# A recurrent decoder step on one core: the samples' own tokens in one product for four heads, the normalizers of four heads together, the sums of squares one step later, and another order inside the residual

## The chip, the core and the metric

The kernel runs on one core of one Trainium2 chip. The metric is the device time of one execution in microseconds; here it is the median of several executions. TensorE (PE) multiplies matrices, VectorE (DVE), ScalarE (ACT) and GpSimd (POOL) work element by element, and SyncE (SP) and POOL issue most of the DMA transfers. Matmuls accumulate in PSUM; all other tiles lie in SBUF. PE has two rows in a profile: PE for matmuls and PEld for loading the stationary operand, which overlaps with them.

## The reference, cut to what matters

One layer of a decoder runs for a prompt of 256 tokens and for 8 sample sequences of 4 tokens each, with shared weights. Three branches run side by side: a linear recurrence (RG-LRU), gated linear attention (GLA, 4 heads) and mLSTM (4 heads); then comes an MLP. Everything is fp32.

```python
xn = rmsnorm(x, g_norm1) * (1.0 + sc1) + sh1
proj = xn @ w_in                       # 2048 -> all branches and the three merge gates
# GLA, per chunk (a sample sequence is one chunk of 4 tokens):
o = einsum(qe, S) + einsum(where(mask, qe @ ke^T, 0), v)
# mLSTM, per chunk:
num = ci * einsum(q, C) + einsum(S, v)
den = ci * einsum(q, n) + sum(S)
h = num / maximum(abs(den), exp(-mt))
merged = gate0 * (y_lru @ w_br_lru) + gate1 * (y_gla @ w_br_gla) + gate2 * (y_ml @ w_br_ml)
x = x + gt1 * (merged @ w_out)
x = x + gt2 * (square(relu(norm2(x) @ w_ff1)) @ w_ff2)
y = rmsnorm(x, g_final)
```

For a sample, the first term of `o` and of `num` (and `den`) reads the sequence's stored state, another one for each of the 8 sequences and 4 heads; the second term is the attention of the 4 new tokens to themselves, called *own tokens* below. `gt1` and `gt2` come, with four more factors, from a product of the conditioning vectors with `w_ada`.

## The kernel before, in words

Activations lie with features on the 128 partitions and tokens along the free axis: 256 prompt tokens and 32 sample tokens, 288 columns in all. Each large product streams its weights from HBM in tiles of 128 x 1024 elements (512 KB). ACT rounds a tile to its high half `hi` (L178), DVE subtracts to get the low half `lo` (L185), and PE runs three single-pass matmuls of 288 columns for each 128x128 block: hi by high activations (L211), hi by low activations (L212), lo by high activations (L213). `stream_` does this; it yields after each weight tile, which is one *group* of 24 such matmuls.

`run` drives such a stream. After each group it does one letter of a pattern set by `every` (its `skip` leaves out so many groups first; the pattern then repeats) and then one step of each generator in the list `side`. `L` loads one *unit*, a slice of `w_ada`, into one of the places named in `slots`; `V` visits: PE multiplies all loaded units (L366, with 32 output partitions for each of four quarters). Both the visit and the side steps are issued on PE behind the group's last matmul. Within these constraints a planner of the compiler sets the order of instructions on each engine; only SP's order is as written. POOL issues the DMAs of the sample states.

Two generators matter here. `gla` runs beside the first gate and merge, `mlstm` beside the second merge (`merge(1)`, 48 groups) and the two streams that make `mo` (16 groups); what is left of `mlstm` runs beside the first gate stream of `merge(2)` (8 groups), whose first branch product needs its result `yml`. Both end in a table `at` of steps, filled by `do(step, function)`.

In both, `pair` handles two loaded tiles of sample states. It makes one product with the states, sixteen PE instructions with each sequence's output on its own quarter of the partitions (L1114, L1517), accumulating in a tile from `longp` (pool `pi`, one buffer). It also adds the own tokens of that head: one matmul on partitions 0 to 31 (L1115 with `asb` in GLA for each head, L1520 with `psb` in mLSTM for each head's first pair). Then `update` forms the new states (L1126 and L1130; L1533 and L1536) in tiles from `misc` (pool `px`, two buffers), and ACT copies the finished output out of PSUM (L1119, L1525) into the tile `os`. A later step, `gather_tokens` (L939, L940), brings it back to features on partitions. In mLSTM, `gather` also spreads each head's normalizer, column 256, over the partitions: DVE multiplies it into an identity (L1544), PE multiplies that by ones (L1546, 32 columns), and DVE copies 32x32 of it into `den` (L1548). `squares` (L1554, L1557) squares the result, `last` prepares `den`, `head_sums` (L924) sums the squares over a head on PE, and DVE and ACT make scaling rows of it (`inv_sqrt`, `head_rows`); `scaled_rows` applies them (L142 on PE, L932 on DVE) and splits y into its halves (L556, L557).

`resid` adds a gated product to the residual: a long DVE instruction for the 256 prompt columns (L1643), a product of 32 sample columns into a small tile (L1646) and its addition (L1648). It is called 16 times behind `w_out` and 32 times in the MLP. In the last block of the MLP its result is squared (L495) and summed by PE (L499, L504), then scaled and written out (L1752, L1756).

Of the kernel before, what the change touches and what calls it, by code (L numbers as in the profile page):

```python
# [11 lines left out]
ALU = mybir.AluOpType  # L12
AX = mybir.AxisListType

P = 128
D = 2048
KT = D // P
NP = 256
NB = 8
TS = 4  # L20
NS = NB * TS
N = NP + NS
# [31 lines left out]
def trunk(ctx, tc, io):  # L54
# [28 lines left out]
    def misc():  # L83
        return px.tile([P, 512], F32, tag="px", name=nm("px"))

    def longp():
        return pi.tile([P, 512], F32, tag="pi", name=nm("pi"))

    def sc(shape, tag, bufs=2):
        return sp.tile(shape, F32, tag=tag, name=nm(tag), bufs=bufs)  # L90
# [14 lines left out]
    ident, eye = C("ident"), C("eye")  # L105
# [156 lines left out]
    def every(p, skip=0):  # L262

        pace.update(every=p.split(), n=-skip)
# [662 lines left out]
    def scaled_rows(y, z, r, h):  # L927
# [4 lines left out]
        V.tensor_tensor(out=z[:, a], in0=z[:, a], in1=p[:, :N].unsqueeze(1).to_broadcast([P, 2, N]), op=ALU.mult)  # L932
        split(y[0][:, a], y[1][:, a], z[:, a])

    def gather_tokens(dst, h, o):

        p = misc()
        for e in range(2):
            T.matmul(p[:, NS * e:NS * e + NS], o[:, e * P:(e + 1) * P], eye, start=True, stop=True)  # L939
        V.tensor_copy(dst[:, 2 * h:2 * h + 2, NP:N], p[:, 0:2 * NS].rearrange("p (e t) -> p e t", e=2))  # L940

    def gla():
# [142 lines left out]
        gn = sc([P, 2], "gn5", 1)  # L1085
        V.tensor_scalar(gn, Pm("gn"), 0.5, None, ALU.mult)
        y = []
        tiles, vxs, pos = {}, {}, {}

        def first():  # L1090
            parts(kp, ks, kr)
# [13 lines left out]
            spread(vxs[h], vp[:, h], half)  # L1105

        def pair(h):
            pos[h] = po = longp()
            ns = (2 * h, 2 * h + 1)
            s4s = [tiles[n][:, 0:1024].rearrange("p (b e) -> p b e", b=4) for n in ns]  # L1110
            for q in (1, 0):
                for j in range(4):
                    b = 4 * q + j
                    T.matmul(po[32 * j:32 * j + 32, 0:256], qm[:, h, NS * b:NS * b + NS], s4s[q][:, j, :], start=q == 1, stop=q == 0, skip_group_check=True)  # L1114
            T.matmul(po[0:32, 0:256], asb[:, h], vs[:, 0:256], start=False, stop=True, skip_group_check=True)  # L1115
            for q, s4 in enumerate(s4s):
                update(h, q, s4)
            pos[h] = sc([P, 257], "os", 1)
            S.copy(pos[h][:, 0:256], po[:, 0:256])  # L1119

        def update(h, q, s4):
            n = 2 * h + q
# [191 lines left out]
    def mlstm():  # L1314
# [161 lines left out]
        mn = sc([P, 2], "gn5", 1)  # L1476
        V.tensor_scalar(mn, Pm("mn"), 0.5, None, ALU.mult)
        sums = row("rr")
        tiles, vxs, pos, sqs, stores = {}, {}, {}, [], []
        v2 = flat(slot(2, F32R))  # L1480
        vx = v2[:, 0:1024].rearrange("p (b e) -> p b e", b=4)
        kps = kp, v2[:, 1024:2048].rearrange("p (h d) -> p h d", h=4)
# [22 lines left out]

        def pair(n):
            h = n // 4
            if n % 4 == 0:
                pos[h] = longp()
            po = pos[h]  # L1510
            s4s = [tiles[n + a].rearrange("p (b d e) -> p b d e", b=2, d=2) for a in range(2)]
            for a in (1, 0):
                q = n % 4 + a
                for i in range(2):
                    for d in range(2):
                        b, j = 2 * q + i, 2 * i + d
                        T.matmul(po[32 * j:32 * j + 32, 0:257], qm[:, 2 * h + d, NS * b:NS * b + NS], s4s[a][:, i, d, :],  # L1517
                                 start=q == 1, stop=q == 2, skip_group_check=True)
            if n % 4 == 0:
                T.matmul(po[0:32, 0:257], psb[:, h], vs, start=False, stop=False, skip_group_check=True)  # L1520
            for a, s4 in enumerate(s4s):
                update(n + a, s4)
            if n % 4:
                pos[h] = sc([P, 257], "os", 1)
                S.copy(pos[h], po[:, 0:257])  # L1525

        def update(n, s4):
            h, q = n // 4, n % 4
# [11 lines left out]

        def gather(h):
            gather_tokens(nT, h, pos[h])
            rd = sc([P, NS], "rd", 1)
            V.tensor_scalar(rd, eye, pos[h][:, 256:257], None, ALU.mult)  # L1544
            p = misc()
            T.matmul(p[:, 0:NS], ones, rd, start=True, stop=True)  # L1546
            r = slice(32 * h, 32 * h + 32)
            V.tensor_copy(den[r, NP:N], p[r, 0:NS])  # L1548

        def squares(h):  # L1550
            if not sqs:
# [9 lines left out]
        def do(s, f, *a):  # L1561
            at.setdefault(s, []).append(lambda: f(*a))
# [28 lines left out]
            V.scalar_tensor_tensor(den, den, EPS, den, ALU.mult, ALU.mult)  # L1591

        do(e + 2, last)
        do(e + 3, lambda: head_sums(sums, sqs[0]))
        do(e + 4, lambda: V.scalar_tensor_tensor(sums, sums, 1.0 / 256, den, ALU.mult, ALU.add))
        rows = []
        do(e + 4, lambda: rows.append(head_rows(inv_sqrt(sums, sums), v2)))
        yield from steps(at)
        while not mos:
            yield  # L1600
# [11 lines left out]

    merge(1, ygla, io["wbg"])
    slots.update(ids=(None, 8), n=0)
    every("L L . V . . .", skip=5)

    mo = slot(3)
    for b in range(2):
# [2 lines left out]
        run(stream(win, B_MO + b, act1, KT, ev_mo))  # L1621
    mos.append(mo)

    visit()
    slots.update(ids=(None, "st", 5), n=0)
    every(". L L L V . .", skip=6)
    merge(2, yml, io["wbm"])


# [10 lines left out]
        return mrg[k // 8][:, k % 8, :], mrg[2 + k // 8][:, k % 8, :]  # L1640

    def resid(x, z, kind, k):
        V.scalar_tensor_tensor(x[:, 0:NP], z[:, 0:NP], mod[:, kind, k, 0:1], x[:, 0:NP], ALU.mult, ALU.add)  # L1643
        t = sc([P, NS], "rs_t", 2)
        bc = [P, NB, TS]
        V.tensor_tensor(out=t.rearrange("p (b t) -> p b t", b=NB), in0=z[:, NP:N].rearrange("p (b t) -> p b t", b=NB),  # L1646
                        in1=mod[:, kind, k, 1:9].unsqueeze(2).to_broadcast(bc), op=ALU.mult)
        V.tensor_tensor(out=x[:, NP:N], in0=x[:, NP:N], in1=t, op=ALU.add)  # L1648

    xf = (slot(6), slot(7))  # L1650
# [227 lines left out]
```

## Time and profile before

| | us |
|---|---|
| median of 3 executions | 1930.77 (1930.58 to 1931.68) |
| the profiled execution | 1930.15 |
| its span, first to last instruction | 1928.0 |
| PE busy | 1907.8 |
| PEld busy | 1823.2 |
| DVE busy | 1035.3 |
| ACT busy | 806.2 |
| POOL busy | 250.4 |

The profiled execution's own time has some 2 us around the span. Busy times of an engine are added over its instructions. Bars of PE overlap, since the ends of matmuls are modelled. The three streaming lines L211 to L213 make up most of PE's time; the units' line L366 and the lines of the three branches are the rest. The groups that the change touches, with their number of instructions, busy us and mean ns:

| line | what | instructions | busy us | mean ns |
|---|---|---|---|---|
| L1115 | GLA's own tokens | 8 | 2.4 | 379 |
| L1520 | mLSTM's own tokens | 8 | 2.4 | 380 |
| L1546 | normalizers | 8 | 1.2 | 232 |
| L924 | sums of squares, both layers | 32 | 2.4 | 412 |

An fp32 matmul appears as two instructions, so four matmuls are eight.

### The profile page before, as it was taken

Reading aid. Unit: us, or ns where it says so; the run is one execution under the profiler, and the core shown is the slowest. Engines: PE = TensorE matmul, PEld = TensorE weight load, DVE = VectorE, ACT = ScalarE, POOL = GpSimd, SP = SyncE. Lnnn points to the kernel's source line nnn. Section 1 sums busy time; section 2 is a strip of 40 time slices with the busy share of each in tenths; the row PEclk is TensorE's granted clock in tenths of the full one; section 3 lists DMA queues with packets and bytes.
Section 4 is the critical chain, followed back from the end, with each engine's and each line's share of the span. In section 5 each row is a group of like instructions: output and inputs, shape, how many; then the busy total and the mean of one; then the engine's idle time right before and its main releaser. Section 6 shows DMA issues by size and latency. Waiting matters only on the chain.

```text
span 1928.0 us, 35983 instructions
## 1 busy us (share of the span) xinstructions
PE 1907.8 (99%) x15092; PEld 1823.2 (95%) x15092; DVE 1035.3 (54%) x1595; ACT 806.2 (42%) x1125; POOL 250.4 (13%) x350
## 2 busy tenths in 40 slices
PE   8999999999999999999999999999999999999997
PEld 6898999999999999899999899999999999999997
DVE  6666647546673456644454654345454544444565
ACT  4333465343554343343333444443333333343433
POOL 0000101021051222001122421010000000000101
PEclk9999999999999999999999999999999999999999
DMA  9997847558443569767788364544444445444452
GB/s 386 389 349 274 313 160 262 202 198 292 163 156 112 174 224 322 270 247 283 277 328 328 132 215 146 172 168 165 169 163 170 165 152 178 166 164 171 156 175 105
DMA packets 110402, 416.42 MB, mean 216 GB/s; under 512 B 11713, under 2 KB 12273, under 8 KB 106529
## 3 DMA queue, kind: packets, MB, share of 16 engines
q1 hardware_dynamic: 100992, 381.40, 55.4%
q0 software_dynamic: 8096, 29.19, 4.2%
q10 hardware_dynamic: 1152, 3.54, 0.5%
q8 instruction: 118, 1.93, 0.4%
q14 instruction: 44, 0.35, 0.1%
HBM read 397.27 MB, written 16.81 MB: 215 GB/s over the span
## 4 chain that ended last, share of the span: by engine, by line
PE 98%; DVE 1%; DMA 1%; ACT 0%; SPq 0%; issue 0%; DVEq 0%; ACTq 0%
PE mm L211 29%; PE mm L213 29%; PE mm L212 29%; PE pa L366 5%; DMA s<-wad 1%; PE px L1533 0%; PE px L769 0%; PE pi L1517 0%; PE px L1052 0%; PE px L1446 0%; PE px L1456 0%; PE mm L248 0%; PE pi L1070 0%; PE px L1126 0%; PE pi L504 0%; PE mm L249 0%
## 5 line engine op out<-in xcount | busy, mean ns | idle before, releaser
L185 DVE TENSOR_TENSOR lo<-raw,hi 128x1024 fp32r<-128x1024 f32 x448 | 548.4, 1226 | 536.5 <-ACT hi L178 514.0
L178 ACT ACTIVATE hi<-raw 128x1024 fp32r<-128x1024 f32 x444 | 470.2, 1060 | 779.6 <-PE mm L212 646.4
L211 PE MATMUL mm<-xh,hi 128*128 128x288 f32 x2528 | 743.9, 298 | 0.1
L212 PE MATMUL mm<-xl,hi 128*128 128x288 f32 x2528 | 741.9, 296 | 0.0
L213 PE MATMUL mm<-xh,lo 128*128 128x288 f32 x2528 | 731.9, 295 | 0.7 <-DVE lo L185 0.6
L211 PE MATMUL mm<-s,hi 128*128 128x288 f32 x1664 | 490.1, 297 | 0.0
L212 PE MATMUL mm<-s,hi 128*128 128x288 f32 x1664 | 488.6, 295 | 0.0
L211 PEld LDWEIGHTS mm<-xh,hi 128*128 128x128 f32 x2528 | 471.6, 188 | 16.2 <-issue 10.5
L213 PE MATMUL mm<-s,lo 128*128 128x288 f32 x1664 | 477.3, 295 | 0.0
L212 PEld LDWEIGHTS mm<-xl,hi 128*128 128x128 f32 x2528 | 474.1, 188 | 1.0
L213 PEld LDWEIGHTS mm<-xh,lo 128*128 128x128 f32 x2528 | 471.1, 188 | 1.7 <-DVE lo L185 1.2
L211 PEld LDWEIGHTS mm<-s,hi 128*128 128x128 f32 x1664 | 311.9, 188 | 4.4 <-issue 3.3
L212 PEld LDWEIGHTS mm<-s,hi 128*128 128x128 f32 x1664 | 312.4, 188 | 0.2
L213 PEld LDWEIGHTS mm<-s,lo 128*128 128x128 f32 x1664 | 308.8, 188 | 0.1
L185 DVE TENSOR_TENSOR lo<-s,hi 128x1024 fp32r<-128x1024 f32 x80 | 98.0, 1225 | 113.4 <-ACT hi L178 113.4
L178 ACT ACTIVATE hi<-s 128x1024 fp32r<-128x1024 f32 x80 | 84.9, 1061 | 142.4 <-PE mm L212 141.7
L1708 POOL TENSOR_TENSOR t<-t 128x288 f32<-128x288 f32 x64 | 60.2, 951 | 639.2 <-ACT t L1707 639.2
L1211 POOL TENSOR_TENSOR s<-s,t 128x288 f32<-128x288 f32 x32 | 36.3, 1161 | 221.2 <-DVE t L1210 221.2
L636 DVE TENSOR_TENSOR s<-s,mm 128x288 f32<-128x288 f32 x92 | 39.9, 451 | 46.6 <-PE mm L213 45.6
L1724 DVE TENSOR_TENSOR s<-s,mm 128x288 f32<-128x288 f32 x96 | 40.3, 450 | 33.9 <-PE mm L213 32.6
L366 PE MATMUL pa<-s,silc 128*32 128x64 f32 (+3 forms) x816 | 47.8, 369 | 0.3 <-DMA s<-wad 0.3
L557 DVE TENSOR_TENSOR s<-t,s 128x288 fp32r<-128x288 f32 x64 | 33.8, 567 | 15.5 <-ACT s L556 15.5
(412 smaller groups left out, 1151.0 us busy)
## 6 DMA issues: line engine op xcount, KB each, us to landing
raw<-win SPq DMA_DIRECT2D x188, 512.0 KB, 4.5
raw<-wf SPq DMA_DIRECT2D x176, 512.0 KB, 4.1
s<-wf SPq DMA_DIRECT2D x80, 512.0 KB, 3.4
s<-wad SPq DMA_DIRECT2D x24, 1024.0 KB, 10.4
s<-wada SPq DMA_DIRECT2D x24, 1024.0 KB, 9.5
ag<-wada SPq DMA_DIRECT2D x21, 1024.0 KB, 6.9
raw<-wout SPq DMA_DIRECT2D x32, 512.0 KB, 5.6
st<-wada SPq DMA_DIRECT2D x26, 512.0 KB, 6.8
```

The source lines that it names most:

```text
L178: pace["hi"] = S.activation(hi, raw, AF.Copy)
L185: pace["lo"] = V.tensor_tensor(out=lo[:, r], in0=raw[:, r], in1=hi[:, r].bitcast(F32), op=ALU.subtract)
L211: T.matmul(pss[m][:, :N], hi[:, kk, ms], xh, start=k == k0 and not take, stop=False)
L212: T.matmul(pss[m][:, :N], hi[:, kk, ms], xl, start=False, stop=False)
L213: pace["last"] = T.matmul(pss[m][:, :N], lo[:, kk, ms], xh, start=False, stop=k == kt - 1 and keep is None)
L366: pace["prod"] = T.matmul(ps[32 * j:32 * j + 32, h * w // 4:(h + 1) * w // 4], silu_c(k), v[:, j], start=k == 0 and h == 0, stop=k == KT - ...
L557: pace["mod"] = V.tensor_tensor(out=dst_l[:, r], in0=src[:, r], in1=dst_h[:, r].bitcast(F32), op=ALU.subtract)
L636: pace["adds"].append(V.tensor_tensor(out=dst[:, base + m, :], in0=dst[:, base + m, :], in1=p, op=ALU.add))
L1211: G.tensor_tensor(out=a, in0=a, in1=t, op=ALU.add)
L1708: G.tensor_tensor(out=r, in0=r, in1=r, op=ALU.mult)
L1724: V.tensor_tensor(out=a, in0=a, in1=p, op=ALU.add)
```

## The change

Five edits:

1. Own tokens. A new helper `own_tokens` multiplies all four heads at once, each on its own quarter of the partitions, in one tile from `misc`, at the first pair; ACT copies that tile into one that takes the place of `vs`. The matmul of each head inside `pair` goes. A new helper `with_own` copies the head's states' product on ACT as before and then lets DVE add the 32 partitions of that head.
2. Normalizers. `rd` holds four heads; the heads' identities are filled one by one as before, and one matmul of 128 columns with four copies follows behind the last head.
3. Sums of squares. `head_sums`, and the rows made of it, come one step later.
4. The units' visit. The last visit of the `mo` streams moves to the first group of `merge(2)`; the loads stay where they were.
5. Residual. The small product of the sample columns comes ahead of the long instruction.

```diff
+    def own_tokens(att, vs, w):
+
+        p = misc()
+        for h in range(4):
+            T.matmul(p[32 * h:32 * h + 32, 0:w], att[:, h], vs[:, 0:w], start=True, stop=True)
+        own = sc([P, 257], "vs", 1)
+        S.copy(own[:, 0:w], p[:, 0:w])
+        return own
+
+    def with_own(po, own, h, w):
+
+        o = sc([P, 257], "os", 1)
+        r = slice(32 * h, 32 * h + 32)
+        S.copy(o[:, 0:w], po[:, 0:w])
+        V.tensor_tensor(out=o[r, 0:w], in0=o[r, 0:w], in1=own[r, 0:w], op=ALU.add)
+        return o
...
         def pair(h):
-            pos[h] = po = longp()
+            if h == 0:
+                owns.append(own_tokens(asb, vs, 256))
+            po = longp()
...
-            T.matmul(po[0:32, 0:256], asb[:, h], vs[:, 0:256], start=False, stop=True, skip_group_check=True)
...
-            pos[h] = sc([P, 257], "os", 1)
-            S.copy(pos[h][:, 0:256], po[:, 0:256])
+            pos[h] = with_own(po, owns[0], h, 256)
...
+            if n == 0:
+                owns.append(own_tokens(psb, vs, 257))
...
-            if n % 4 == 0:
-                T.matmul(po[0:32, 0:257], psb[:, h], vs, start=False, stop=False, skip_group_check=True)
...
-                pos[h] = sc([P, 257], "os", 1)
-                S.copy(pos[h], po[:, 0:257])
+                pos[h] = with_own(po, owns[0], h, 257)
...
-            rd = sc([P, NS], "rd", 1)
-            V.tensor_scalar(rd, eye, pos[h][:, 256:257], None, ALU.mult)
+            V.tensor_scalar(rd[:, h], eye, pos[h][:, 256:257], None, ALU.mult)
+            if h < 3:
+                return
             p = misc()
-            T.matmul(p[:, 0:NS], ones, rd, start=True, stop=True)
-            r = slice(32 * h, 32 * h + 32)
-            V.tensor_copy(den[r, NP:N], p[r, 0:NS])
+            T.matmul(p[:, 0:P], ones, rd.rearrange("p h i -> p (h i)"), start=True, stop=True)
+            for i in range(4):
+                r = slice(32 * i, 32 * i + 32)
+                V.tensor_copy(den[r, NP:N], p[r, NS * i:NS * i + NS])
...
-        do(e + 3, lambda: head_sums(sums, sqs[0]))
-        do(e + 4, lambda: V.scalar_tensor_tensor(sums, sums, 1.0 / 256, den, ALU.mult, ALU.add))
+        do(e + 4, lambda: head_sums(sums, sqs[0]))
+        do(e + 5, lambda: V.scalar_tensor_tensor(sums, sums, 1.0 / 256, den, ALU.mult, ALU.add))
         rows = []
-        do(e + 4, lambda: rows.append(head_rows(inv_sqrt(sums, sums), v2)))
+        do(e + 5, lambda: rows.append(head_rows(inv_sqrt(sums, sums), v2)))
...
-    every("L L . V . . .", skip=5)
+    every("L L . V . . . L L . . . . .", skip=5)
...
-    visit()
     slots.update(ids=(None, "st", 5), n=0)
-    every(". L L L V . .", skip=6)
+    every("V . . . . . " + 9 * ". L L L V . . ")
     merge(2, yml, io["wbm"])
...
     def resid(x, z, kind, k):
-        V.scalar_tensor_tensor(x[:, 0:NP], z[:, 0:NP], mod[:, kind, k, 0:1], x[:, 0:NP], ALU.mult, ALU.add)
         t = sc([P, NS], "rs_t", 2)
...
+        V.scalar_tensor_tensor(x[:, 0:NP], z[:, 0:NP], mod[:, kind, k, 0:1], x[:, 0:NP], ALU.mult, ALU.add)
         V.tensor_tensor(out=x[:, NP:N], in0=x[:, NP:N], in1=t, op=ALU.add)
```

## What is expected, and why

> **What bounds the kernel now.** I read the page first (busy times, then the chain that ended last), then the busy time by stretches, then the waits of PE. Columns of a stretch row: from:to in us, length, then busy us of PE, PEld, DVE, ACT and POOL with instruction counts, granted clock, DMA share, GB/s.
>
> ```profile
> span 1928.0 us, 35983 instructions
> PE 98%; DVE 1%; DMA 1%; ACT 0%; SPq 0%; issue 0%; DVEq 0%; ACTq 0%
> ```
>
> ```profile
> 426.00:490.00 64.00, 64.00 (x519) 57.83 (x518) 39.24 (x67) 27.30 (x42) 7.86 (x16) 1.00 0.78 274
> 690.00:805.00 115.00, 115.00 (x940) 104.58 (x939) 73.65 (x155) 45.12 (x62) 20.94 (x33) 1.00 0.86 297
> 1096.00:1913.70 817.70, 817.70 (x6142) 815.76 (x6140) 408.12 (x531) 334.09 (x446) 81.84 (x99) 1.00 0.48 164
> 1913.70:1928.00 14.30, 2.43 (x9) 1.27 (x8) 7.97 (x20) 1.73 (x5) 0.00 (x0) 0.69 0.43 165
> ```
>
> 98% of the chain is PE. In the stretch of the GLA states (426 to 490), in that of the mLSTM states (690 to 805) and in the feed-forward part PE is busy all the time, at granted clock 1.00, while DVE has a third or more to spare. So in these stretches an edit is worth just what it takes out of, or puts into, PE's row of instructions; work on DVE, ACT, POOL and DMA counts only if PE is made to wait. From 1913.7 on, PE is nearly done and a latency chain counts instead.
>
> PE's busy sum overlaps (a matmul's end is modelled), so I price by distance from one start to the next. A streaming matmul (288 columns) starts 0.13 us after the one before it (rows of Part 2: 798.66, then 798.79).
>
> **Part 1, the samples' own tokens.** The old code has four matmuls in GLA (L1115) and four in mLSTM (L1520), each alone on 32 output partitions behind the sixteen instructions that run on all four quarters (an fp32 matmul shows as two instructions). In mLSTM every head has one group of states with that matmul and one without, which is a direct comparison (columns: start us, us, what):
>
> ```profile
> 691.85 0.29 PE L213 MATMUL mm<-xh,lo 128*128 128x288 f32 x1
> 692.07 1.07 PE L1517 MATMUL pi<-st,s 128*32 128x257 f32 x16
> 692.97 0.60 PE L1520 MATMUL pi<-vs,gks 128*32 128x257 f32 x2
> 693.49 0.50 PE L1533 MATMUL px<-s,s 128*128 128x256 f32 x2
> ...
> 694.07 0.29 PE L213 MATMUL mm<-xh,lo 128*128 128x288 f32 x1
> ```
>
> The group without it, between the sixteen and the next streaming matmul the same two L1533 pairs:
>
> ```profile
> 702.73 1.07 PE L1517 MATMUL pi<-s,s 128*32 128x257 f32 x16
> ...
> 704.32 0.30 PE L211 MATMUL mm<-xh,hi 128*128 128x288 f32 x1
> ```
>
> With it the group takes 694.07 - 692.07 = 2.00 us, without it 704.32 - 702.73 = 1.59. One such matmul is worth 0.41, not the 0.60 of its bar and not the 0.52 to the next start: about 0.1 of that is the end of a 32-wide run, which moves to the sixteen. GLA's group is built alike:
>
> ```profile
> 427.48 1.05 PE L1114 MATMUL pi<-st,s 128*32 128x256 f32 x16
> 428.34 0.59 PE L1115 MATMUL pi<-vs,s 128*32 128x256 f32 x2
> 428.87 0.74 PE L1126 MATMUL px<-s,s 128*128 128x256 f32 x4
> ```
>
> Its matmul takes 0.53 to the next start; less the same 0.1 that is 0.42; I take 0.41 for all. Removed: 8 x 0.41 = 3.3 us.
>
> Added: four matmuls once in each layer, one on each quarter, eight instructions. The nearest rows are the sixteen on four quarters: 428.34 - 427.48 = 0.86, or 0.054 each, and 692.97 - 692.07 = 0.90. So 0.43 and 0.45 if they stand directly in front of the sixteen, where the code puts them: 0.9. Standing alone they would pay for entering (692.07 - 691.85 = 0.22 instead of 0.13) and for leaving, some 0.3 a place, 0.6 in all. I take 0.9 and keep 1.5 as an end. Net: 2.4 (end 1.8). If a matmul's full 0.53 fell away, removal would be 4.2 and the net 3.3: the upper end.
>
> The Trainium skill, page "TensorE: Matmul & The Clock Gate", section "Part 3: Packing small matmuls — row/col tiling", measured 2.38 times the speed for three column tiles; carried to four as an estimate, that is 3.2 times, so that the eight instructions would take 4 x 0.41 / 3.2 = 0.5 each time and the sum would be 0.2 smaller. The trace has 0.054 on four quarters against 0.41 / 2 = 0.2 on one, nearly four times, and decides.
>
> Beside PE: ACT copies the result once in each layer, and DVE adds it for each of the eight heads. Two rows of ACT, and the nearest of DVE:
>
> ```profile
> 692.05 1.06 ACT L178 ACTIVATE hi<-raw 128x1024 fp32r<-128x1024 f32 x1 [3.60 <-PE mm L212]
> 703.88 0.38 ACT L1525 COPY os<-pi 128x257 f32<-128x257 f32 x1
> ```
>
> ```profile
> 800.00 0.65 DVE L1557 TENSOR_SCALAR s<-s,gn 128x288 f32<-128x288 f32 x2 [0.64 <-ACT s L1554]
> ```
>
> The copy is like L1525, 0.38. The trace has no such add; L1557 scales 128x288 twice in 0.65, so 0.33 each, and an add with two inputs is unlikely to need twice that: from 0.3 to 0.65 each, 5.2 us at the most for eight, in 179 us in which DVE is idle for 66. The gathering that waits for the add is issued a step or more later, a group of 24 streaming matmuls (3.2 us). Cost taken: nothing; if that cover were gone, the copy and the add (0.4 + 0.3 to 0.65) would show as PE idle before the gathering. The add waits for ACT, and behind it in DVE's queue stands the next `lo`, whose weights PE uses a group or more later; so PE is the one that would wait for it, and 3.2 us cover the 0.4. What can bite is the copy: see the second rival.
>
> **Part 2, the normalizers.** Four fp32 matmuls of 32 columns (L1546) become one of 128.
>
> ```profile
> 798.66 0.29 PE L213 MATMUL mm<-xh,lo 128*128 128x288 f32 x1
> 798.79 0.30 PE L1546 MATMUL px<-rd,ones 128*128 128x32 f32 x2
> 798.93 0.38 PE L211 MATMUL mm<-xh,hi 128*128 128x288 f32 x1
> 799.14 0.29 PE L212 MATMUL mm<-xl,hi 128*128 128x288 f32 x1
> ```
>
> ```profile
> 565.24 1.95 PE L1354 MATMUL px<-s,s 128*128 128x128 f32 x16
> 566.94 0.38 PE L211 MATMUL mm<-s,hi 128*128 128x288 f32 x1
> ```
>
> Each takes 0.14, and the next streaming matmul needs 0.21 instead of 0.13: 0.22, four of them 0.88. A 128-column one: L1354 has 1.70 / 16 = 0.106 an instruction, so 0.21, and the same 0.08 behind it: 0.29. Saved: 0.6. DVE's four copies of 32x32 now come together at the end, under 1 us, with the denominator wanted only after the sums of squares. Hidden.
>
> **Part 3, the units' visit and the sums of squares.** Both go one step (one group) later, in the first group of the third gate instead of the last group of `mo`. What is moved is PE's visit of two units and L924, and behind these the row chain (DVE, ACT) and y. No DMA is issued by it.
>
> ```profile
> 799.89 1.06 PE L366 MATMUL pa<-ag,silc 128*32 128x512 f32 x8
> 800.77 1.04 PE L366 MATMUL pa<-s,silc 128*32 128x512 f32 x8
> 801.75 0.40 PE L211 MATMUL mm<-xh,hi 128*128 128x288 f32 x1
> 801.98 0.30 PE L212 MATMUL mm<-xl,hi 128*128 128x288 f32 x1
> ...
> 802.74 1.18 PE L924 MATMUL px<-s,ones 128*32 128x288 f32 x16
> ```
>
> Behind them, SP's next load into the `ag` slot, DVE's split of head 0's y, and PE's first use of y:
>
> ```profile
> 812.39 0.43 SPq L405 DMA_DIRECT2D ag<-wada  x1
> ```
>
> ```profile
> 815.43 1.42 DVE L557 TENSOR_TENSOR s<-s,s 128x576 fp32r<-128x576 f32 x2
> ```
>
> ```profile
> 829.82 0.30 PE L211 MATMUL mm<-s,hi 128*128 128x288 f32 x1
> ```
>
> Now both are 32-wide runs with some streaming matmuls between (1 us). The squares came just then (ACT L1554 released DVE's L1557 at 800.00, Part 1); a step later they are long done, so L924 can follow the visit at once. Saved: the last unit's longer end (0.98 against 0.88), the slower first matmul (0.23 against 0.13) and the slower entry (0.22 against 0.13, Part 1): 0.3; nothing if they stay apart. What is late next: the `ag` slot is read until about 805 instead of 801.75, and SP asks for it at 812.39: 7 us to spare, so weights queued behind it on SP aren't held. Head 0's y is split by 816.85 and first used at 829.82: 13 us to spare, of which a group takes 3.2.
>
> **Part 4, the residual's order.** 48 calls, three DVE instructions each as before. PE waits for none of them until the tail:
>
> ```profile
> 1912.16 0.48 DVE L1643 SCALAR_TENSOR_TENSOR s<-mm,mod,s 128x256 f32<-128x256 f32 x1 [3.21 <-PE mm L213]
> ...
> 1913.18 0.18 DVE L1648 TENSOR_TENSOR s<-s,rs_t 128x32 f32<-128x32 f32 x1
> ```
>
> ```profile
> 1913.95 2.42 PE L504 MATMUL pi<-t,ones 128*128 128x288 f32 x8 [0.24 <-ACT t L495]
> ```
>
> Feature block 12's long instruction starts at 1912.16, its add only at 1913.18: 1.0 later, though 0.48 and a product of 32 columns (the add's size, 0.18) stand before it, so the next block's long instruction went in between. With the small product first, the add can follow the long instruction: 1912.16 + 0.18 + 0.48 = 1912.8, some 0.4 sooner, and its square too. PE's idle 0.24 goes, and no more than that: the eight instructions behind are dense. Saved: 0.24, or 0 if the order on DVE stays mixed.
>
> **Sum.** 2.4 + 0.6 + 0.3 + 0.24 = 3.6 us (3.57 before rounding). Against the profiled execution (1930.15 us, of which the span is 1928.0) that gives 1926.6; the median shown is 0.6 above that execution, so 1930.77 - 3.6 = **1927.2 us**. By the ends: least 1.8 + 0.6 = 2.4, so 1928.4; most 3.3 + 0.6 + 0.3 + 0.24 = 4.5, so 1926.3.
>
> **The rivals.** (a) *The larger saving.* The matmul on one quarter costs its full 0.53 wherever it stands, and PE gets more from the denser order: 4.5 us, 1926.3. For it: the bars of L1115 and L1520. Against it: the comparison inside mLSTM, with and without.
>
> (b) *A wait takes the place.* The own product takes one of the two px buffers just as the update of the states needs both. The update's second product then waits for ACT's copy, which may stand behind a `hi` (1.06): 1.06 + 0.38 = 1.4 at each of two places, 2.9 us, leaving 0.7: 1930.1. For it: ACT's queue is in order, and a `hi` starts at the very moment of that group (692.05). Against it: ACT waits before most `hi` (3.60 there), so it has room, and streaming matmuls can be placed in between, as they are now. The Trainium skill, page "TensorEngine Tiling (Array Packing)", section "PSUM Bottleneck", speaks for this one: after a fourfold speedup on TensorE the PSUM copy may become the bound. No row here shows PE held by such a copy.
>
> (c) *Slower.* The row chain behind the sums of squares slips and y is late at the third branch product. Place: 829.82. PE loses one for one whatever goes beyond the 13 us; the result is over 0.2% slower than before from 13 + 3.6 + 3.9 = 20.5 us of lateness. If the heads' y fell behind the whole gate block (8 groups of 3.2 = 25.6 us), PE would idle 12.6 and the time be 1939.8. For it: that chain is moved, alternates with `lo` on DVE, and its steps now end in the sixth of the block's eight groups instead of the fifth. Against it: one group is a quarter of the margin.
>
> **How the numbers follow.** Forecast 0.74, (a) 0.11, (b) 0.10, (c) 0.05. About 0.2%, or 3.9 us, is what a measurement can tell from no change: the line is at 1926.9, just below my number. Of the forecast's 0.74 I put 0.24 below it. Faster: 0.24 + 0.11 = 0.35. Within: 0.50 + 0.10 = 0.60. Slower: 0.05. The range runs from 1925.5 (rival (a) and the spread of the shown times, about 1 us) to 1929.8: it holds the forecast with its ends, most of (a), and (b) at one place.
>
> **What would show it.** Right: no 32-wide pair behind the sixteen (2.00 becomes 1.59), eight instructions in 0.43 to 0.45 before the first group; one L1546 of 128 columns; L924's line directly behind L366; no idle before L504 at the end. Wrong: an idle PE at the update behind the own product (b), a wait at the first product with y (c), or streams elsewhere ordered differently by more than the 3.6 us in question.

## The result, and the profile after

The changed kernel takes **1926.44 us** (median of 12 runs), the kernel before 1930.67 us in the 12 runs beside it: a ratio of 0.9979, 95% interval 0.9971 to 0.9986. The profiled execution took 1926.27 us against 1930.15, and its span 1924.2 us against 1928.0: 3.8 us less. The forecast was 1927.2 with a range from 1925.5 to 1929.8. The time lies in it; the saving, 4.2 us in medians, is 0.6 more than the 3.6 of the sum. It also lies below 1926.9, where the prediction drew its line for a time that can be told from before, and to that side it had given 0.35 against 0.60 for no clear difference. One of the 12 runs took 7970 us and one of the 33 runs of the kernel before beside e1 to e4 took 6167 us, without a trace that shows why, and without the first of them the median is 1926.41.

The page of the changed kernel: its span and the chain that ended last.

```profile
span 1924.2 us, 35993 instructions
...
PE 98%; DVE 1%; DMA 0%; ACT 0%; issue 0%; SPq 0%; DVEq 0%; ACTq 0%
```

PE carries 98% of the chain, as before. The busy time by stretches, with the columns and the bounds of the view of before:

```profile
426.00:490.00 64.00, 64.00 (x528) 58.44 (x527) 42.01 (x72) 28.86 (x44) 7.87 (x16) 1.00 0.79 279
690.00:805.00 115.00, 115.00 (x950) 105.58 (x950) 76.14 (x159) 46.84 (x64) 20.16 (x32) 1.00 0.88 299
```

PE is busy for all of both stretches in both kernels, but it now fits 528 instructions into the first and not 519, and 950 into the second and not 940. A busy time of 100% tells nothing of a saving: the saving shows as *where the same instruction starts*. So I cut both timelines of PE at four instructions that both kernels have, and at the end of the last L504. After:

```profile
304.12 1.07 PE L366 MATMUL pa<-st,silc 128*32 128x256 f32 x16
...
564.14 1.95 PE L1371 MATMUL px<-s,s 128*128 128x128 f32 x16
...
836.15 1.07 PE L366 MATMUL pa<-ag,silc 128*32 128x512 f32 x8
...
1182.36 1.07 PE L366 MATMUL pa<-s,silc 128*32 128x512 f32 x8
...
1910.27 2.22 PE L504 MATMUL pi<-t,ones 128*128 128x288 f32 x8
```

Before (the row of the second cut, L1354 at 565.24, and that of the last, L504 at 1913.95 for 2.42 us, stand in the prediction):

```profile
303.94 1.07 PE L366 MATMUL pa<-st,silc 128*32 128x256 f32 x16
...
839.49 1.06 PE L366 MATMUL pa<-ag,silc 128*32 128x512 f32 x8
...
1185.68 1.07 PE L366 MATMUL pa<-s,silc 128*32 128x512 f32 x8
```

The differences of these times give the length of each stretch in us, and what the change takes out of it:

| stretch (its content) | before | after | saved |
|---|---|---|---|
| A: 304 to 565 (GLA and its states) | 261.30 | 260.02 | 1.28 |
| B: 565 to 839 (mLSTM, its states, normalizers, sums) | 274.25 | 272.01 | 2.24 |
| C: 839 to 1185 | 346.19 | 346.21 | -0.02 |
| D: 1185 to the end of the last L504 (feed-forward, last residual, tail) | 730.69 | 730.13 | 0.56 |
| together | 1612.43 | 1608.37 | 4.06 |

The empty row C tells something too: 16 of the 48 residual calls fall into it, with their new order, and nothing is gained there. The experiments are read by the same cuts, since their differences of tenths of a us are near the 0.1% by which medians can be told apart.

### The profile page after: what moved, and what is told of

It is laid out like the page before. It is cut to its first block, busy times and chain, and to the rows that moved or that the text cites. A ratio compares the mean times of both kernels' runs of the same rounds, so it can differ in the third digit from the quotient of the medians.

```text
span 1924.2 us, 35993 instructions
## 1 busy us (share of the span) xinstructions
PE 1904.2 (99%) x15086; PEld 1821.5 (95%) x15086; DVE 1039.7 (54%) x1603; ACT 807.2 (42%) x1127; POOL 251.3 (13%) x350
## 3 DMA queue, kind: packets, MB, share of 16 engines
q10 hardware_dynamic: 1152, 3.54, 0.5%
## 4 chain that ended last, share of the span: by engine, by line
PE 98%; DVE 1%; DMA 0%; ACT 0%; issue 0%; SPq 0%; DVEq 0%; ACTq 0%
PE mm L211 29%; PE mm L213 29%; PE mm L212 29%; PE pa L366 5%; PE px L1550 0%; PE px L769 0%; PE pi L1537 0%; PE px L1069 0%; PE px L1463 0%; DMA s<-x 0%; PE px L1473 0%; PE mm L248 0%; PE pi L1087 0%; PE px L1143 0%; PE mm L249 0%; PE pi L570 0%
## 5 line engine op out<-in xcount | busy, mean ns | idle before, releaser
L211 PE MATMUL mm<-xh,hi 128*128 128x288 f32 x2528 | 743.2, 298 | 0.1
L212 PE MATMUL mm<-xl,hi 128*128 128x288 f32 x2528 | 742.2, 296 | 0.0
L211 PE MATMUL mm<-s,hi 128*128 128x288 f32 x1664 | 490.8, 297 | 0.0
L212 PE MATMUL mm<-s,hi 128*128 128x288 f32 x1664 | 489.3, 295 | 0.0
L211 PEld LDWEIGHTS mm<-xh,hi 128*128 128x128 f32 x2528 | 471.6, 188 | 14.5 <-issue 9.8
L212 PEld LDWEIGHTS mm<-xl,hi 128*128 128x128 f32 x2528 | 474.2, 188 | 1.4 <-issue 0.5
L211 PEld LDWEIGHTS mm<-s,hi 128*128 128x128 f32 x1664 | 312.0, 188 | 4.3 <-issue 3.3
L212 PEld LDWEIGHTS mm<-s,hi 128*128 128x128 f32 x1664 | 312.5, 188 | 0.3
```

The costliest lines, as they stand in the source:

```text
L211: T.matmul(pss[m][:, :N], hi[:, kk, ms], xh, start=k == k0 and not take, stop=False)
L212: T.matmul(pss[m][:, :N], hi[:, kk, ms], xl, start=False, stop=False)
```

## The experiments

Each kernel is the changed one with one thing undone or one thing added, apart from one that is the kernel before with one part of the change. Savings are against the kernel before, by the cuts above; the differences from the changed kernel are what the undone part is worth. Medians and ratios are against runs of the kernel before on the same chip.

| kernel | median us (before beside it) | ratio, 95% interval | A | B | C | D | sum |
|---|---|---|---|---|---|---|---|
| the change, first profile | 1926.44 (1930.67) | 0.9979, 0.9971 to 0.9986 | 1.28 | 2.24 | -0.02 | 0.56 | 4.06 |
| the change again (e10) | 1926.81 (1930.50) | 0.9979, 0.9969 to 0.9989 | 1.28 | 2.19 | -0.02 | 0.56 | 4.01 |
| own tokens as before (e1) | 1928.75 (1930.34) | 0.9992, 0.9984 to 1.0001 | -0.01 | 0.96 | -0.02 | 0.57 | 1.50 |
| own tokens standing alone (e5) | 1926.75 (1930.25) | 0.9984, 0.9975 to 0.9993 | 0.95 | 1.90 | -0.03 | 0.57 | 3.39 |
| normalizers as before (e2) | 1926.91 (1930.34) | 0.9983, 0.9974 to 0.9992 | 1.28 | 1.54 | -0.02 | 0.56 | 3.36 |
| visit and sums as before (e3) | 1927.56 (1930.34) | 0.9986, 0.9977 to 0.9995 | 1.28 | -0.32 | -0.03 | 0.56 | 1.49 |
| visit alone as before (e11) | 1926.92 (1930.50) | 0.9978, 0.9970 to 0.9987 | 1.28 | 1.86 | -0.02 | 0.57 | 3.69 |
| residual as before (e4) | 1927.02 (1930.34) | 0.9984, 0.9975 to 0.9993 | 1.28 | 1.53 | -0.02 | 0.00 | 2.79 |
| residual's order alone (e8) | 1929.44 (1930.25) | 0.9995, 0.9987 to 1.0004 | 0.01 | 0.00 | -0.01 | 0.56 | 0.56 |
| copy eight times (e6) | 1927.15 (1930.25) | 0.9988, 0.9979 to 0.9997 | 1.27 | 0.46 | -0.02 | 0.56 | 2.27 |
| rows four groups later (e7) | 1926.48 (1930.25) | 0.9980, 0.9971 to 0.9989 | 1.28 | 2.07 | -0.02 | 0.56 | 3.89 |

A first use of the table: the two profiles of the changed kernel agree to 0.05 in each stretch, so an effect of 0.1 us can be read from one profile. In B this holds only where PE shows no wait for weights: the profiles of e3 and e4 have such waits, which cost 1.4 and 0.65 us (below and in the last section). The two medians of the changed kernel, on different chips, differ by 0.37.

**e1, own tokens as before.** The four matmuls of each layer go back into the heads' groups.

```diff
-            if n == 0:
-                owns.append(own_tokens(psb, vs, 257))
...
+            if n % 4 == 0:
+                T.matmul(po[0:32, 0:257], psb[:, h], vs, start=False, stop=False, skip_group_check=True)
...
-                pos[h] = with_own(po, owns[0], h, 257)
+                pos[h] = sc([P, 257], "os", 1)
+                S.copy(pos[h], po[:, 0:257])
```

(and likewise in GLA).

> The changed kernel with part 1 alone undone: each head's own tokens again as one matmul on 32 partitions behind the sixteen, no common product, no addition on DVE. Prediction's term: 2.4 us slower than the changed kernel's 1926.4, so 1928.8. Rival (a), a matmul's full 0.53 us falls away: 3.3 us slower, 1929.7. A rival that gives the gain to the order of the rest of the program: under 1 us slower. In the trace the first group of an mLSTM head should take 2.00 us again instead of 1.59, and the common product's 0.43 to 0.46 us be gone.

Measured: A falls from 1.28 to -0.01 and B from 2.24 to 0.96: 1.29 and 1.28, together 2.57. C and D don't move. The pair of rows that does it, PE of e1:

```profile
692.49 1.07 PE L1535 MATMUL pi<-st,s 128*32 128x257 f32 x16
693.38 0.60 PE L1538 MATMUL pi<-vs,gks 128*32 128x257 f32 x2
...
694.25 0.40 PE L1551 MATMUL px<-s 128*128 128x256 f32 x2
694.48 0.29 PE L213 MATMUL mm<-xh,lo 128*128 128x288 f32 x1
```

and PE of the changed kernel, first head and second:

```profile
690.76 0.29 PE L213 MATMUL mm<-xh,lo 128*128 128x288 f32 x1
690.98 0.64 PE L939 MATMUL px<-vs,gks 128*32 128x257 f32 x8
691.44 1.05 PE L1537 MATMUL pi<-st,s 128*32 128x257 f32 x16
...
713.82 1.07 PE L1537 MATMUL pi<-st,s 128*32 128x257 f32 x16
...
715.16 0.29 PE L211 MATMUL mm<-xh,hi 128*128 128x288 f32 x1
```

The reader is to see three things. The group with its pair on one quarter still takes 694.48 - 692.49 = 1.99 in e1. In the changed kernel the pair is gone: the sixteen and the first update product take 715.16 - 713.82 = 1.34, and the second product, which here stands further on, the same 0.23 as in e1 (694.48 - 694.25); together 1.57. And the eight new instructions take 691.44 - 690.98 = 0.46, with nothing paid for entering, since the 0.22 from 690.76 to 690.98 was paid by the sixteen before. That is four times 0.42 less 0.46, or 1.2 of the measured 1.28 in one layer. The eight instructions of four quarters take nearly what two on one quarter took (0.41): nearly four times the speed. The single starts in the trace show how: the eight come in two sets of four, each set within 0.02, the second set 0.24 behind the first; the two of L1520 in the kernel before start 0.22 apart. So four instructions on four quarters take the time of one on one quarter. DVE's new addition (L949) takes 0.41, inside the 0.3 to 0.65 of the prediction, and PE shows no wait for it. The Trainium skill, page "TensorE: Matmul & The Clock Gate", section "Part 3: Packing small matmuls — row/col tiling", has 2.38 times for three column tiles; the extension to four that the prediction weighed (0.5 each time) is not what this kernel shows.

**e5, own tokens standing alone.** The same eight instructions, a step earlier, away from the sixteen.

```diff
-            if n == 0:
-                owns.append(own_tokens(psb, vs, 257))
...
+        do(4, lambda: owns.append(own_tokens(psb, vs, 257)))
```

(in GLA likewise, at step 3).

> The changed kernel with the common product of the own tokens one step (mLSTM) or one step (GLA) earlier, away from the sixteen. Prediction's price for standing apart: 0.3 us at each of two places, so 0.6 slower than the changed kernel, 1927.0. If neighbours don't matter: no difference. In the trace: 0.22 us before the eight instructions instead of 0.13, about 0.1 more at their end and 0.1 more on the next streaming matmul.

Measured: A loses 0.33 and B 0.34. PE of e5 shows where:

```profile
686.20 0.29 PE L213 MATMUL mm<-s,lo 128*128 128x288 f32 x1
686.42 0.64 PE L939 MATMUL px<-vs,gks 128*32 128x257 f32 x8
686.99 0.40 PE L211 MATMUL mm<-xh,hi 128*128 128x288 f32 x1
687.23 0.30 PE L212 MATMUL mm<-xl,hi 128*128 128x288 f32 x1
```

Entering 0.22 instead of 0.13, the eight 0.57 instead of 0.46, and 0.24 instead of 0.13 to the second streaming matmul: 0.09 + 0.11 + 0.11 = 0.31 for a run of 32-wide matmuls that has no other beside it. So the place in front of the sixteen is worth 0.67 in the two layers; it is part of the gain, as the prediction's end of 1.5 instead of 0.9 had it.

**e6, the copy eight times.** Rival (b) said that ACT's copy of the own product holds one of two px buffers while the update needs both. The copy is made eight times longer.

```diff
-        S.copy(own[:, 0:w], p[:, 0:w])
+        for _ in range(8):
+            S.copy(own[:, 0:w], p[:, 0:w])
```

> The changed kernel with ACT's copy of the common product done eight times over, so that the product holds its px buffer about 2.7 us longer and ACT is 2.7 us later with its next work, at two places. Rival (b) of the prediction, that this copy is on PE's path: up to 2 x 2.7 = 5.4 us slower. Prediction: the copy is covered, at most 0.3 us slower; the planner puts streaming matmuls in between and PE shows no wait there.

Measured: A is as with one copy (1.27); B loses 1.78, where at most 0.3 was expected. ACT, PE and POOL of e6, in this order:

```profile
695.44 0.76 ACT L942 COPY vs<-px 128x257 f32<-128x257 f32 x2
```

```profile
697.21 0.39 PE L1551 MATMUL px<-s 128*128 128x256 f32 x2
...
715.36 1.07 PE L1538 MATMUL pi<-st,s 128*32 128x257 f32 x16 [1.56 <-DMA st<-mC]
```

```profile
708.80 0.54 POOL L1519 DMA_DIRECT2D st<-mC  x1 [4.88 <-DMA o_C_s<-st]
```

So the expectation failed. The mechanism of the rival is there, but its price falls in another place. The last of the eight copies ends at 695.44 + 0.76 = 696.20, and the second update product stands behind it in PE's order: it starts at 697.21, where the changed kernel has it at 694.49. PE doesn't idle there, because streaming matmuls stand in between. What is late is the store of the new states on POOL and then the reload of the buffer with the next states, which waits for that store, and PE pays 1.56 at 715.36, 18 us on. With one copy PE has no such wait. POOL of the changed kernel:

```profile
705.49 0.53 POOL L1518 DMA_DIRECT2D st<-mC  x1 [3.63 <-DMA o_C_s<-st]
```

In the changed kernel this reload lands 4.4 us after its start, at 709.9, and PE needs it at 713.82: 3.9 us to spare. In e6 the store is 2.7 later (702.74 against 700.01), the reload starts 3.3 later and takes 6.4 to land, at 715.2. So a copy that ended some 3.9 us later (696.20, against 691.92 + 0.35 = 692.27 in the changed kernel) has become a landing 5.3 us later; why the reload also took longer was not tried. The Trainium skill, page "TensorEngine Tiling (Array Packing)", section "PSUM Bottleneck", warns that the copy from PSUM may become the bound; with one copy it doesn't here, and with eight it does through a queue. Where between one and eight it begins was not tried.

**e2, normalizers as before.** One matmul of 32 columns for each head.

```diff
-            if h < 3:
-                return
             p = misc()
-            T.matmul(p[:, 0:P], ones, rd.rearrange("p h i -> p (h i)"), start=True, stop=True)
-            for i in range(4):
...
+            T.matmul(p[:, 0:NS], ones, rd[:, h], start=True, stop=True)
+            r = slice(32 * h, 32 * h + 32)
+            V.tensor_copy(den[r, NP:N], p[r, 0:NS])
```

> The changed kernel with part 2 alone undone: one 32-column matmul and one copy for each head's normalizer. Prediction's term: 0.59 us slower, so 1927.0. By the changed kernel's trace, where the pair of 128 columns takes 0.13 us and not 0.21: 0.66 slower. If PE's cost were the columns alone (4 x 32 = 128 either way): no difference.

Measured: B loses 0.70, all else stays. PE of the changed kernel:

```profile
796.99 0.38 PE L1564 MATMUL px<-rd,ones 128*128 128x128 f32 x2
797.12 0.38 PE L211 MATMUL mm<-xh,hi 128*128 128x288 f32 x1
797.34 0.29 PE L212 MATMUL mm<-xl,hi 128*128 128x288 f32 x1
```

The pair of 128 columns takes 0.13 to the next start, not the 0.21 I gave it: as much as a pair of 32 columns took (0.14 at 798.79 before). Four such places less one are 3 x 0.22 = 0.66, near the 0.70. That four times the columns cost nothing here is why one matmul for all heads is worth three places. How the 0.21 came about, the end of the sixteen L1354 of the prediction shows:

```profile
566.68 0.50 PE L1354 MATMUL px<-s,s 128*128 128x128 f32 x3
```

One of these has a bar of 0.27, so the three start 0.11 apart, the last at 566.91, and the streaming matmul behind them starts at 566.94: the last one costs 0.03. Sixteen are fifteen distances of 0.11 and one of 0.03, or 1.70; two are one of each, or 0.14. The mean of a long run, 0.106, doesn't hold for a run of two.

**e3, visit and sums of squares as before**, and **e11, the visit alone as before.** In e3 the sums go back to step e+3 and the visit into the last group of `mo`; in e11 only the visit does, and the sums keep their new step, so that the two stand apart.

```diff
-    every("L L . V . . . L L . . . . .", skip=5)
+    every("L L . V . . .", skip=5)
...
+    visit()
...
-    every("V . . . . . " + 9 * ". L L L V . . ")
+    every(". L L L V . .", skip=6)
```

and in e3 also

```diff
-        do(e + 4, lambda: head_sums(sums, sqs[0]))
+        do(e + 3, lambda: head_sums(sums, sqs[0]))
```

(with the two lines behind it from e+5 to e+4).

> The changed kernel with parts 3 and 4 of the edits undone: the visit of two units and the sums of squares in the last group of the mo streams, as before. Prediction's term: 0.3 us slower, so 1926.75, with streaming matmuls again between the visit and the sums. If only the position counts and not that the two stand together: no difference.

> The changed kernel with the units' visit back in the last group of the mo streams, the sums of squares staying one step later: only their standing together is undone, and the sums are not put where their squares are just being made. Prediction's term for Part 3: 0.3 us slower than the changed kernel. If it is the place of the visit that counts: as much as undoing both, 1 us or more slower.

Measured: e11 loses 0.38 in B. e3 loses 2.56 there in its profile, while its median gains 2.78 on the kernel before (1930.34 - 1927.56), 1.45 less than the change's 4.23. PE of the changed kernel, where the three runs stand as one:

```profile
801.02 1.07 PE L366 MATMUL pa<-ag,silc 128*32 128x512 f32 x8
801.90 1.04 PE L366 MATMUL pa<-s,silc 128*32 128x512 f32 x8
802.76 1.15 PE L924 MATMUL px<-s,ones 128*32 128x288 f32 x16
803.85 0.40 PE L212 MATMUL mm<-xl,hi 128*128 128x288 f32 x1
```

The second unit takes 0.86 instead of the 0.98 of before, and L924 enters without the 0.09 and the slow first matmul: 0.12 + 0.10 + 0.09 = 0.31, by e11 0.38; the last 0.07 has no row of its own. PE of e3:

```profile
789.07 0.29 PE L213 MATMUL mm<-xh,lo 128*128 128x288 f32 x1
...
790.77 0.40 PE L213 MATMUL mm<-xh,lo 128*128 128x288 f32 x1 [0.73 <-DVE lo L185]
...
801.59 0.69 PE L924 MATMUL px<-s,ones 128*32 128x288 f32 x6
...
802.79 1.16 PE L924 MATMUL px<-s,ones 128*32 128x288 f32 x10
```

Two things are in e3 that the edit did not intend. L924 is split in two runs, six and ten, so one more place of some 0.33 is paid (the price from e5). The split also breaks up the sets of four: in the changed kernel the sixteen start in four sets, at 802.76, 803.00, 803.25 and 803.49, in e3 in six, at 801.59, 801.86, 802.79, 803.06, 803.30 and 803.54, the last two of them a single instruction each. Two sets more at 0.24 are 0.48. And weights come late: from 789.07 to 790.77, a distance of three starts, are 1.70 instead of 0.40, and some 0.1 more goes to the slower matmul at 790.77 (0.40): 1.4 lost, ahead of everything that the edit touches. 0.38 + 0.33 + 0.48 + 1.4 = 2.6, which is the 2.56. So e3 alone doesn't price Part 3, since the kernel before has its sixteen in one run; e11 does, for the part that the prediction priced.

**e4, the residual as before**, and **e8, the residual's order alone** (the kernel before with this one part). In `resid` the long product stands first again, or in e8 second.

```diff
+        V.scalar_tensor_tensor(x[:, 0:NP], z[:, 0:NP], mod[:, kind, k, 0:1], x[:, 0:NP], ALU.mult, ALU.add)
         t = sc([P, NS], "rs_t", 2)
...
-        V.scalar_tensor_tensor(x[:, 0:NP], z[:, 0:NP], mod[:, kind, k, 0:1], x[:, 0:NP], ALU.mult, ALU.add)
```

> The changed kernel with the residual's old order. Prediction's term: 0.24 us slower, the idle before the last sums of squares and nothing else. By the changed kernel's trace, where the eight matmuls of those sums also take 2.22 us and not 2.42 and start 0.13 us behind the last streaming matmul: 0.4 to 0.6 us slower, all of it behind the last streaming matmul. If the 48 calls cost PE something elsewhere: a difference at the end of the output product, ahead of the MLP.

> The kernel before with the residual's new order alone. Prediction's term: 0.24 us faster than before, 1930.4. By the changed kernel's trace: 0.4 to 0.6 us faster, 1930.1 to 1930.3, with the same dense end as there. With the run that undoes this part it shows whether the parts add up.

Measured: in D, e4 loses all of the 0.56 and e8 alone gains all of it. In A, B and C e8 moves nothing by more than 0.01: of 48 calls only those at the tail count. (e4's B is 0.71 lower too; that is a late weight at 790.18, not the edit: see the last section.) PE at the tail: of before, then of e8.

```profile
1913.41 0.29 PE L213 MATMUL mm<-s,lo 128*128 128x288 f32 x1
```

```profile
1913.56 0.29 PE L213 MATMUL mm<-s,lo 128*128 128x288 f32 x1
1913.69 2.22 PE L504 MATMUL pi<-t,ones 128*128 128x288 f32 x8
```

DVE and ACT of the changed kernel there:

```profile
1908.32 0.47 DVE L1665 SCALAR_TENSOR_TENSOR s<-mm,mod,s 128x256 f32<-128x256 f32 x1
1908.71 0.18 DVE L1666 TENSOR_TENSOR s<-s,rs_t 128x32 f32<-128x32 f32 x1
```

```profile
1911.24 0.44 ACT L495 ACTIVATE t<-s 128x288 f32<-128x288 f32 x1 [0.35 <-DVE s L1666]
```

The mechanism is the one forecast: feature block 12's add starts 0.39 behind its long instruction, not 1.0. With it came something that was not forecast: the planner also put PE's last streaming matmuls in another order, so block 12's product is complete sooner. Its first DVE instruction starts 1.25 before the last streaming matmul begins in the kernel before (1912.16 and 1913.41), and 1.92 before it in e8 (1911.64 and 1913.56). So e8 prices both together. The size is not the one forecast. In the kernel before, L504 starts 1913.95 - 1913.41 = 0.54 behind the last streaming matmul, in e8 0.13: 0.41 gained, where the profile gives 0.24 as the idle time. The difference is the modelled end of the last streaming matmul, 1913.41 + 0.29 = 1913.70, against 0.13 between two starts in a dense stream. And the eight L504 were 2.42 and are 2.22, another 0.20. 0.41 + 0.20 = 0.61, of which D keeps 0.56, since its last streaming matmul is 0.05 later against the cut at 1185. The eight aren't dense either: the last pair needs k = 15's square, which ends at 1911.24 + 0.44 = 1911.68, and the pair can't begin sooner.

**e7, the rows four groups later.** Rival (c) lets y be late at the third branch product. The row chain behind the sums goes from step e+5 to e+9.

```diff
-        do(e + 5, lambda: rows.append(head_rows(inv_sqrt(sums, sums), v2)))
+        do(e + 9, lambda: rows.append(head_rows(inv_sqrt(sums, sums), v2)))
```

(and the line of `sums` before it.)

> The changed kernel with the rows made of the sums of squares four groups later than the change has them (the sums themselves stay), so y of each head is 4 x 3.2 = 12.8 us later. By rival (c)'s arithmetic head 0's y has 13.0 us of margin before the change, of which the change takes 3.2: 9.8 are left, so PE should idle about 3.0 us before the first branch product with y, and the time be 1929.4. If the margin is larger than that (the planner puts other work there): no difference. If the later heads decide, whose y then comes at the end of the gate block: more than 3 us.

Measured: 0.17 lost in B, no more. DVE and PE of e7:

```profile
825.78 0.76 DVE L557 TENSOR_TENSOR s<-s,s 128x576 fp32r<-128x576 f32 x1 [1.07 <-ACT s L556]
```

```profile
826.28 0.56 PE L211 MATMUL mm<-s,hi 128*128 128x288 f32 x3
826.67 0.33 PE L212 MATMUL mm<-s,hi 128*128 128x288 f32 x1
```

Head 0's split is now an instruction by itself, done at 825.78 + 0.76 = 826.54, and PE has three L211 ahead of the first L212, at 826.67. PE shows no wait there. What was off is the delay. DVE's first instruction of the moved rows in e7, which the changed kernel has at 804.55:

```profile
811.83 0.45 DVE L1614 SCALAR_TENSOR_TENSOR row<-row,row 128x288 f32<-128x288 f32 x1
```

Four steps more in the program are 7.3 us here, not 12.8. Head 0's split ends 10.5 later than in the changed kernel (826.54 against 816.03, the first of its two splits at 815.28). There PE first uses y at 826.48, so head 0 has 10.4 us to spare, and e7 uses up just that. The prediction's 13 less 3.2 is 9.8, counted from the end of two heads' splits. So the margin was about right, and the delay of e7 was too small to go beyond it: what PE loses beyond the margin is not shown.

**e10, the change again,** beside e11 on one chip, for the spread of a profile.

> The changed kernel once more, as the reference for the run beside it and for how much one execution differs from the next. Prediction from the twelve runs so far: 1926.4. If weights that land late in the mo streams (0.4 to 1.2 us of waiting in two of the other runs' profiles, none in this kernel's first one) belong to its normal course, its times should spread by more than 1 us.

By the cuts it saves 4.01, against 4.06 in the first profile. Its median is 1926.81, 0.4 above the expected 1926.4, and its times run from 1925.97 to 1928.49, so they spread by more than 1 us. That doesn't show late weights to be at work: the kernel before spreads from 1930.08 to 1933.58 beside it, and this profile has no such wait.

## Why the prediction held, point by point

- **What bounds the kernel**: right. All of the gain is in PE's starts; e8 changes the order of three DVE instructions in 48 calls and gains only at the tail, where the prediction had placed it.
- **Part 1, 2.4 us**: measured 1.29 + 1.28 = 2.57 (e1). The price of a matmul on one quarter from the comparison inside mLSTM (0.41) and the sum of 0.9 for the new eight hold: 0.43 in GLA and 0.46 in mLSTM. The end of 1.5 for standing alone holds too: e5 pays 0.67 where 0.6 was expected. GLA's row of the eight:

```profile
427.67 0.62 PE L939 MATMUL px<-vs,s 128*32 128x256 f32 x8
428.10 1.05 PE L1133 MATMUL pi<-st,s 128*32 128x256 f32 x16
```

- **Part 2, 0.6**: measured 0.70 (e2). The term "L1354 has 0.106 an instruction, so 0.21" was off: 0.13. The mean over sixteen was used for a run of two: by the starts in the same row it would have been 0.11 + 0.03 = 0.14. The pair of 32 columns takes 0.14 as well; why the width costs nothing was not tried further.
- **Part 3, 0.3**: measured 0.38 (e11). The order came as forecast, L924 right behind the visit. PE shows no wait behind it.
- **Part 4, 0.24**: measured 0.56 (e4 and e8). This is the step that failed, in size: "PE's idle 0.24 goes, and no more than that: the eight instructions behind are dense". The idle time was taken from a modelled end, while everywhere else I had priced by starts; by starts it was 0.54 less 0.13. And the eight were not dense: 2.42 became 2.22. So PE gained 0.41 ahead of the eight and 0.20 in them, and not 0.24; part of what made the squares early was a new order of PE's last streaming matmuls, which the prediction didn't have.
- **The sum**: 2.57 + 0.70 + 0.38 + 0.56 = 4.2 from the parts undone one by one, 4.06 in the cuts of the change and 3.8 in the span (the first cut itself lies 0.18 later). The median gained 4.2. The prediction's own terms, 2.4 + 0.6 + 0.3 + 0.24, add up to 3.54 and not 3.57, which leaves its 1927.2 as it is.
- **Rival (a)**, a larger saving because the matmul on one quarter costs its full 0.53: not so (e1: 2.57, not 3.3). Of the 0.6 to 0.7 by which the parts exceed the sum, Part 4 has 0.32 and Part 1 0.17; Parts 2 and 3 have 0.1 each. All four terms came out too small, so nothing offset Part 4.
- **Rival (b)**, the copy: not at work in the change. e6 shows that it can be: with eight copies, when the next states land 5.3 us later than in the changed kernel, which has 3.9 us to spare there. It then costs PE a wait for a DMA 18 us later and not one at the update.
- **Rival (c)**, y late: not at work. In the changed kernel head 0's y has 10.4 us to spare, near the 9.8 of the prediction, and e7's delay of 10.5 us shows no wait.

## What to carry to other kernels

Price by starts on a bound engine, also where it idles: an idle time of the profile counts from a modelled end and was 0.24 where 0.41 was to be gained. Take the cost of a short run from single starts, not from the mean of a long one: two of L1354 would be 0.14 by their starts, and 0.21 by the mean. Small matmuls on one quarter of the array were worth gathering in fours here, and most where another 32-wide run stands directly behind them: the same eight instructions cost 0.46 there and 0.77 by themselves. A buffer that is held too long need not stop the engine that asks for it; look for its price at the next load into whatever the delayed work was to free, and compare when that load lands with when it is needed.

## What was not expected of the hardware

- **The width of a short fp32 matmul**: 128 columns and 32 took the same 0.13 to 0.14 to the next start (796.99 and 798.79), with 0.22 and 0.21 for the matmul behind.
- **Weights with little to spare.** In 690 to 805 the DMA share is 0.86 before and 0.88 after, at 297 and 299 GB/s. The profile of e4 has PE wait there for a weight:

```profile
789.50 0.29 PE L212 MATMUL mm<-xl,hi 128*128 128x288 f32 x1
790.18 0.40 PE L213 MATMUL mm<-xh,lo 128*128 128x288 f32 x1 [0.39 <-DVE lo L185]
```

  From 789.50 to 790.18 are 0.68 instead of 0.13, and 0.1 more behind it: 0.65 of the 0.71 that e4 lacks in B. The edit of e4 touches nothing that runs there. Of the twelve profiles only those of e3 and e4 have this wait. In both, one and the same load of weights is late. ACT, which rounds this tile first, waits for it in the changed kernel too, and in e3 longer:

```profile
786.71 1.06 ACT L178 ACTIVATE hi<-raw 128x1024 fp32r<-128x1024 f32 x1 [5.29 <-DMA raw<-win]
```

```profile
788.40 1.06 ACT L178 ACTIVATE hi<-raw 128x1024 fp32r<-128x1024 f32 x1 [7.04 <-DMA raw<-win]
```

  In e4 the same instruction starts at 787.81. The load is issued between 771.4 and 772.0 in all three and takes 14.6 us to land in the changed kernel, 16.1 in e4 and 16.8 in e3, where the page of the kernel before has 4.5 for the median of these loads. So 1.1 us of additional lateness is enough for PE to wait here. Whether the shorter stretch of the changed kernel brings PE nearer to that wait is only argued; it stays open, as does how often it happens.
